# Key and value weights' low parts on VectorE, and the first pair's maxima behind twenty k-steps of the values

## The chip, the cores and the metric

The kernel runs on one core of a Trainium2 chip. The metric is the device time of one execution in microseconds, the median of several runs. The engines are named as in the profile: PE is TensorE (matrix products), PEld its weight loads, DVE is VectorE, ACT is ScalarE, POOL is GpSimd, SP is SyncE, which here issues all loads and stores (DMAs).

## What is computed

Two layers of a diffusion backbone over 512 latent tokens (`L`) and 256 context tokens (`C`), width 1024. Layer 0 mixes tokens by grouped-query attention (16 query heads of 64, 4 heads for keys and values, norm on queries and keys, rotary positions on the latent part); layer 1 by a two-way state-space scan. Each mixer is followed by a gated feed-forward network with a short convolution. The change touches layer 0's attention alone:

```python
q_l, k_l, v_l = jnp.split(h_lat @ w_qkv, [Q_DIM, Q_DIM + KV_DIM], axis=-1)
q_l = rms_norm(q_l.reshape(bsz, seq, N_HEADS, HEAD_DIM), q_norm)
k_l = rms_norm(k_l.reshape(bsz, seq, N_KV_HEADS, HEAD_DIM), k_norm)
...
q_l = apply_rope(q_l, cos, sin)
k_l = apply_rope(k_l, cos, sin)
...
s = jnp.einsum('bqhgd,bkhd->bhgqk', q, k).astype(jnp.float32) * (HEAD_DIM ** -0.5)
p = jax.nn.softmax(s, axis=-1).astype(v.dtype)
return jnp.einsum('bhgqk,bkhd->bqhgd', p, v)
```

## The kernel before

**Products in three parts.** A float32 operand is split into a high part (a rounded copy, type float32r) and a low part (what is left). A product of two operands is three products on PE: high by high, high by low, low by high. `split` (L81) makes the parts: the high one is a cast on ScalarE (L85), the low one a subtraction (L87) on VectorE, or on GpSimd where the caller says `lo_engine="pool"`. `load_w` (L90) loads a block of weights (L95) and splits it; `pin=True` keeps the two instructions in the order in which they are written.

**The stages of the attention.** `attention` runs in this order. (1) Queries and keys of the latent tokens for the first six heads' pairs, tiles `ps_l`. (2) The same for the context, six groups of 24 products, tiles `ps_c`, each copied to `raw0` to `raw5` by ScalarE (L821): `raw0` are the first keys, `raw1` the first queries, `raw2`, `raw4`, `raw5` the next queries, `raw3` the second keys. In between, the two blocks of the values' weights are loaded and split into `wh` and `wl` on ScalarE and GpSimd (L823), and the first keys and queries are prepared. (3) The values: six tiles `ps_v` of 8 k-steps, a k-step being three products (L620); 48 k-steps in all. (4) Eight pairs of query heads, seven steps each: scores (`ps_s`, L796), their shift (L798, with a diagonal matrix `diag` of the row maxima), the exponential on ScalarE (`pr`, L799), sums of `pr` on VectorE (`acc`), and the product with the values (`ps_o`, L760). The next pair's maxima, the next queries' projection (`ps_q`), the modulation (`ps_ada`) and the output projection are woven between these steps.

**Preparing keys and queries.** `normed` (L628 on) squares on ScalarE (L631), scales (L632), sends a copy with swapped rows through a DMA (`qsw`, L635, four loads), sums the squares over a head by products with ones (`ssq`, L640), applies the rotation on VectorE (L642 to L644), and, behind a `yield`, the root (`qy`, L649 and L650 on ScalarE) and the norm (L653 to L655 on VectorE). `keys` (L660) then writes, for each of two heads, tiles `kh` and `kl` in which both halves of 64 partitions hold the same head: `kh` by two casts on ScalarE (L666, L667), `kl` by a subtraction on VectorE for one half (L668) and a cast of it on ScalarE for the other (L669). `queries` (L674) splits into `qh` and `ql`.

**The maxima.** `Pair.maxima` (L714) makes products `ps_m` (L724) in seven groups; VectorE takes each group's maximum (L726, `ma` and `mb`), joins them (L742) and builds `diag` (L747). Without it the shift L798 of the pair's scores cannot run.

**What sets the order.** Each engine works through its own queue in order. From stage 2 on, the queues' order is made by a scheduling layer from the order of the code and its own estimates; an instruction moves ahead of another where nothing binds them, unless it is kept in program order or an edge without a semaphore is added (`add_manual_dep`, as in `follow`). In stage 3 a loop over the 48 k-steps (at the end of `attention`) issues a group of maxima (`m`) every fifth k-step from the first and a part of the second query (`qfirst`) every sixth. PSUM holds two double banks (tag `S`: `ps_s`, `ps_m`) and four single ones (tag `B`: `ps_c`, `ssq`, `ps_v`, `ps_q` and others), so a tile waits until the one that held its bank is read. Weight blocks share ten buffers (`t4`).

Of the kernel before, what the change touches and what calls it, by code (L numbers as in the profile page):

```python
# [7 lines left out]
P = 128  # L8
# [3 lines left out]
ALU = mybir.AluOpType  # L12
# [4 lines left out]
KT = D // P  # L17
# [3 lines left out]
HD = 64  # L21
# [54 lines left out]
def _r(ap):  # L76

    return ap.bitcast(F32)
# [167 lines left out]
def follow(g, bi):  # L246

    if g.last_act is not None:
        g.tc.add_manual_dep(bi.ins, g.last_act.ins.name, mybir.DependencyInfo(
            mybir.DependencyClass.NoSync, mybir.DependencyReason.DATA), reason="order of tables")  # L250
    g.last_act = bi


def ln_exp(g):
# [228 lines left out]
def attention(g, adas, project, X):  # L483


    nc, I = g.nc, g.I
    S64 = slice(0, 64), slice(64, 128)
# [48 lines left out]
    for m in range(KT):  # L536
        sq = t2("sql") if m else acc
# [71 lines left out]
    wv = []  # L609
    vt = [g.t3p.tile([P, NKV * HD], F32, name=f"v{t}") for t in range(T // P)]  # L610

    def values():
        for t in range(T // P):
            h, c0 = (hl, t * P) if t < 4 else (hc, t * P - L)
            ps = Bk("ps_v")
            for k in range(KT):
                w = tuple(w[:, (k % 4) * 256 : (k % 4 + 1) * 256] for w in wv[k // 4])
                ah, al = (a[:, c0 : c0 + P] for a in h[k])
                for i, (s, mv) in enumerate(((ah, w[0]), (ah, w[1]), (al, w[0]))):
                    nc.tensor.matmul(ps[:, :256], s, mv, start=k == 0 and i == 0, stop=k == KT - 1 and i == 2)  # L620
                yield 0.32
            nc.scalar.copy(vt[t], ps[:, :256])

# [4 lines left out]
    def normed(qs, gain):  # L628

        sq = t3(g, "qsq")  # L630
        nc.scalar.activation(sq, qs, AF.Square)  # L631
        nc.scalar.activation(qs, qs, AF.Identity, scale=gain)  # L632
        sw = t2("qsw")
        for b in range(4):
            nc.sync.dma_start(sw[32 * (b ^ 1) : 32 * (b ^ 1) + 32], qs[32 * b : 32 * b + 32, :L])  # L635
        ss = []
        for c0, c1 in ((0, L), (L, T)):
            ps = Bk("ssq")
            for s in S64:
                nc.tensor.matmul(ps[s, : c1 - c0], g.ones[s, :HD], sq[s, c0:c1], start=True, stop=True)  # L640
            ss.append((ps[:, : c1 - c0], slice(c0, c1)))
        nc.vector.tensor_tensor(qs[:, :L], qs[:, :L], g.cos, ALU.mult)  # L642
        nc.vector.tensor_tensor(sw, sw, g.sin, ALU.mult)
        nc.vector.tensor_tensor(qs[:, :L], qs[:, :L], sw, ALU.add)  # L644
        yield

        y, u = t3(g, "qy"), sq
        for ps, c in ss:
            nc.scalar.activation(y[:, c], ps, AF.Ln, scale=1.0 / HD, bias=eps64)  # L649
        nc.scalar.activation(y, y, AF.Exp, scale=-0.5)  # L650
        nc.scalar.activation(u, y, AF.Square)
        for ps, c in ss:
            nc.vector.scalar_tensor_tensor(u[:, c], ps, HD * EPS, u[:, c], ALU.add, ALU.mult)  # L653
        nc.vector.tensor_tensor(qs, qs, y, ALU.mult)
        nc.vector.scalar_tensor_tensor(qs, u, -3.0 * HD, qs, ALU.add, ALU.mult)  # L655
        yield
# [3 lines left out]
    def keys(j, qs):  # L660
        yield from normed(qs, kn)
        for e in range(2):

            h, l = t3(g, f"kh{j}{e}", F32R), t3(g, f"kl{j}{e}", F32R)
            s, o = S64[e], S64[1 - e]
            nc.scalar.copy(h[s], qs[s])  # L666
            nc.scalar.copy(h[o], qs[s])  # L667
            nc.vector.tensor_tensor(l[s], qs[s], _r(h)[s], ALU.subtract)  # L668
            nc.scalar.copy(l[o], _r(l)[s])  # L669
            k2[2 * j + e] = (h, l)  # L670

    qprep = {}
# [34 lines left out]
    class Pair:  # L707
# [6 lines left out]
        def maxima(self):  # L714
# [5 lines left out]
            def scores(ts, k0, n, out):  # L720
                ps = Sb("ps_m")
                for i, t in enumerate(ts):
                    for e in range(2):
                        nc.tensor.matmul(ps[:, 512 * e + n * i : 512 * e + n * i + n], qh[S64[e], t * P : (t + 1) * P],  # L724
                                         kh[S64[e], k0 : k0 + n], start=True, stop=True)
                nc.vector.reduce_max(out[:, :, ts[0] : ts[-1] + 1], ps.rearrange("p (e t k) -> p e t k", e=2, k=n),  # L726
                                     axis=AX.X, negate=True)

# [88 lines left out]
    for n, j in enumerate((0, 1, 2, 4, 5, 3)):  # L817
        ps = Bk("ps_c")
        for k in range(KT):
            k_step(k, j, ps[:, :C], hc)  # L820
        nc.scalar.copy(raw[j][:, L:], ps[:, :C])  # L821
        if n in (1, 3):
            wv.append(load_w(g, I["wv"][len(wv)], lo_engine="pool", pin=True))  # L823
        if n in (1, 2):
            early.append(keys(0, raw[0]) if n == 1 else queries(0, lambda: raw[1]))
        for gen in early:
            next(gen, None)
# [84 lines left out]
    jobs[4].start()  # L912
    m = pairs[0].maxima()
    for i, _ in enumerate(vals):
        if i % 5 == 0:
            next(m, None)
        if i % 6 == 5:
            next(qfirst, None)
        if i == 20:
            wq_split(4)  # L920
# [714 lines left out]
```

## Time and profile before

| | us |
|---|---|
| median of 3 runs | 1904.47 |
| lowest and highest run | 1903.81, 1907.48 |
| the profiled execution | 1906.4 |
| its span, first to last instruction | 1904.2 |
| DVE busy in the span | 1331.0 (70%) |
| ACT busy in the span | 845.4 (44%) |
| POOL busy in the span | 256.9 (13%) |

The profiled execution is one run with the hardware profiler on. All times of single instructions below are from it, in microseconds from the start of the span. A row of a timeline gives start, duration, engine, line of the kernel, operation, output and inputs, shape, count, and in brackets the idle time of the engine before it with what ended it. A row `PE a <- ACT b: 5.5, 1, 5.5` among the waits says that PE waited for ACT before `a`: sum, number, longest. In a table of stretches stand the stretch, its length, each engine's busy time with its count of instructions, the clock that TensorE was granted (1.00 is full) and the DMA's share and GB/s. Matrix products overlap, so their durations add up to more than the time that passes; their distance from start to start is what counts.

The values' stage lies between 91 and 122 us of the span. The second keys (`raw3`) are prepared at about 210 us, among the steps of the third pair.

### The profile page before, as it was taken

Reading aid. Unit: us, or ns where it says so; the run is one execution under the profiler, and the core shown is the slowest. Engines: PE = TensorE matmul, PEld = TensorE weight load, DVE = VectorE, ACT = ScalarE, POOL = GpSimd, SP = SyncE. Lnnn points to the kernel's source line nnn. Section 1 sums busy time; section 2 is a strip of 40 time slices with the busy share of each in tenths; the row PEclk is TensorE's granted clock in tenths of the full one; section 3 lists DMA queues with packets and bytes.
Section 4 is the critical chain, followed back from the end, with each engine's and each line's share of the span. In section 5 each row is a group of like instructions: output and inputs, shape, how many; then the busy total and the mean of one; then the engine's idle time right before and its main releaser. Section 6 shows DMA issues by size and latency. Waiting matters only on the chain.

```text
span 1904.2 us, 27262 instructions
## 1 busy us (share of the span) xinstructions
PE 1864.1 (98%) x10696; PEld 1528.8 (80%) x10696; DVE 1331.0 (70%) x1983; ACT 845.4 (44%) x1454; POOL 256.9 (13%) x238
## 2 busy tenths in 40 slices
PE   8899999989999999999999999999999999999999
PEld 6774545578888888888888888888888888888887
DVE  4478889678877777544478777777878576565555
ACT  3645544355122222222256767766677352323331
POOL 2300000031000000000040334443334200000000
PEclk8999999999999999999999999999999999999999
DMA  9123341014334556221222344344343323323332
GB/s 339 56 67 97 118 157 40 23 56 166 122 122 133 163 189 186 72 67 56 67 89 80 116 122 122 114 131 123 116 130 119 100 78 101 101 86 111 89 99 89
DMA packets 73424, 210.00 MB, mean 110 GB/s; under 512 B 8912, under 2 KB 14416, under 8 KB 73168
## 3 DMA queue, kind: packets, MB, share of 16 engines
q1 hardware_dynamic: 73296, 208.26, 35.1%
q8 instruction: 84, 1.38, 0.3%
q14 instruction: 44, 0.36, 0.1%
HBM read 198.79 MB, written 6.82 MB: 108 GB/s over the span
## 4 chain that ended last, share of the span: by engine, by line
PE 79%; DVE 9%; issue 3%; ACT 3%; DMA 1%; POOL 1%; SPq 0%; DVEq 0%; POOLq 0%; ACTq 0%
PE ps_up L105 10%; PE ps_up L106 10%; PE ps_up L108 10%; PE ps_d L105 6%; PE ps_d L108 6%; PE ps_d L106 6%; PE ps_in L108 4%; PE ps_in L106 4%; PE ps_in L105 4%; PE ps_o L760 2%; PE ps_s L796 2%; PE ps_st L1222 2%; DVE ht L312 1%; PE ps_wo L108 1%; PE ps_wo L105 1%
## 5 line engine op out<-in xcount | busy, mean ns | idle before, releaser
L87 DVE TENSOR_TENSOR wl<-wst,wh 128x1024 fp32r<-128x1024 f32 x209 | 260.3, 1245 | 227.7 <-PE ps_up L106 121.6
L85 ACT CAST wh<-wst 128x1024 fp32r<-128x1024 f32 x211 | 221.2, 1049 | 422.0 <-DMA wst<-in_wup 321.6
L106 PE MATMUL ps_up<-hlf,wh 128*128 128x512 f32 x1008 | 357.2, 354 | 0.0
L108 PE MATMUL ps_up<-hhf,wl 128*128 128x512 f32 x1008 | 356.9, 354 | 0.0
L105 PE MATMUL ps_up<-hhf,wh 128*128 128x512 f32 x1008 | 356.7, 354 | 0.0
L105 PEld LDWEIGHTS ps_up<-hhf,wh 128*128 128x128 f32 x1008 | 190.6, 189 | 26.5
L106 PEld LDWEIGHTS ps_up<-hlf,wh 128*128 128x128 f32 x1008 | 190.7, 189 | 26.3
L108 PEld LDWEIGHTS ps_up<-hhf,wl 128*128 128x128 f32 x1008 | 190.6, 189 | 26.4
L105 PE MATMUL ps_in<-hhs,wh 128*128 128x512 f32 (+1 forms) x560 | 204.5, 365 | 0.0
L106 PE MATMUL ps_in<-hls,wh 128*128 128x512 f32 (+1 forms) x560 | 199.5, 356 | 0.0
L108 PE MATMUL ps_in<-hhs,wl 128*128 128x512 f32 (+1 forms) x560 | 198.8, 355 | 0.0
L105 PE MATMUL ps_d<-hdh,wh 128*128 128x512 f32 (+1 forms) x568 | 193.6, 343 | 1.4 <-DVE X L970 1.2
L108 PE MATMUL ps_d<-hdh,wl 128*128 128x512 f32 (+1 forms) x568 | 193.4, 341 | 0.0
L106 PE MATMUL ps_d<-hdl,wh 128*128 128x512 f32 (+1 forms) x568 | 193.0, 340 | 0.3 <-DVE hdl L87 0.3
L970 DVE SCALAR_TENSOR_TENSOR X<-ps_d,mod,X 128x512 f32<-128x512 f32 (+1 forms) x224 | 125.0, 584 | 34.1 <-PE ps_d L108 33.8
L106 PEld LDWEIGHTS ps_d<-hdl,wh 128*128 128x128 f32 x568 | 106.7, 188 | 14.8 <-DVE hdl L87 0.7
L105 PEld LDWEIGHTS ps_d<-hdh,wh 128*128 128x128 f32 x568 | 106.3, 188 | 14.8 <-DVE X L970 1.4
L105 PEld LDWEIGHTS ps_in<-hhs,wh 128*128 128x128 f32 x560 | 106.0, 189 | 15.1 <-issue 0.9
L108 PEld LDWEIGHTS ps_in<-hhs,wl 128*128 128x128 f32 x560 | 105.9, 189 | 14.8
L108 PEld LDWEIGHTS ps_d<-hdh,wl 128*128 128x128 f32 x568 | 106.7, 188 | 13.1
L106 PEld LDWEIGHTS ps_in<-hls,wh 128*128 128x128 f32 x560 | 106.0, 189 | 13.2
L799 ACT ACTIVATE pr<-ps_s 128x1024 f32<-128x1024 f32 x56 | 57.1, 1020 | 94.0 <-PE ps_s L798 86.7
(355 smaller groups left out, 3506.4 us busy)
## 6 DMA issues: line engine op xcount, KB each, us to landing
wst<-in_wup SPq DMA_DIRECT2D x88, 512.0 KB, 3.6
wada<-in_adaT SPq DMA_DIRECT2D x56, 512.0 KB, 3.7
wst<-in_win SPq DMA_DIRECT2D x48, 512.0 KB, 3.7
wst<-in_wdown SPq DMA_DIRECT2D x44, 512.0 KB, 3.7
E<-ad SPq DMA_DIRECT2D x64, 256.0 KB, 6.7
wada<-in_adaB SPq DMA_DIRECT2D x24, 512.0 KB, 5.0
ec<-ead SPq DMA_DIRECT2D x64, 128.0 KB, 5.1
wst<-in_wout SPq DMA_DIRECT2D x16, 512.0 KB, 3.6
```

The lines of the kernel that those rows point to most:

```text
L85: keep(nc.scalar.copy(hi, src))
L87: keep(eng.tensor_tensor(lo, src, _r(hi), ALU.subtract))
L105: mm(out, wh, ah, start=first, stop=False)
L106: mm(out, wh, al, start=False, stop=False)
L108: mm(out, wl, ah, start=False, stop=last)
L312: nc.vector.scalar_tensor_tensor(t[:, c0:c1], ap, g.moda[layer][ca][:, m, v : v + 1], rs[:, c0:c1], ALU.mult, ALU.mult)
L760: nc.tensor.matmul(po[S64[e], :n], v, pr[:, 512 * e + off : 512 * e + off + n], start=first, stop=last)
L796: nc.tensor.matmul(outs[e], a[S64[e], k], b[S64[e], q], start=i == 0, stop=False)
L799: nc.scalar.activation(pr, ps, AF.Exp)
L970: nc.vector.scalar_tensor_tensor(ap, o[:, c0:c1], gate[:, m, v : v + 1], ap, ALU.mult, ALU.add)
L1222: nc.tensor.matmul(ps[:, d * 256 : (d + 1) * 256], Bt[:, t * P : (t + 1) * P], xw[d][t], start=t == ts[0], stop=t == ts[-1])
```

## The change

Four things are altered. (1) The low parts of the two blocks of the values' weights are made by VectorE and no longer by GpSimd. (2) The second half of each `kl` is made by VectorE from the same sources as the first (one more subtraction, written to the other 64 partitions) and no longer copied by ScalarE; this holds for the first keys and for the second ones. (3) In the values' loop the groups of maxima begin at k-step 19 and come every third k-step, and the parts of the second query begin at k-step 20 and come every seventh. (4) A function `ordered` ties the first pair's `ps_m` and each `ssq` behind the values' product that was issued last in the code; the tie is one of order on PE and adds no semaphore.

```diff
+def ordered(g, bi, prev):
+
+    if prev is not None:
+        g.tc.add_manual_dep(bi.ins, prev.ins.name, mybir.DependencyInfo(
+            mybir.DependencyClass.NoSync, mybir.DependencyReason.DATA), reason="place among products")
...
+    placed = [None]
+
     def values():
...
-                    nc.tensor.matmul(ps[:, :256], s, mv, start=k == 0 and i == 0, stop=k == KT - 1 and i == 2)
+                    placed[0] = nc.tensor.matmul(ps[:, :256], s, mv, start=k == 0 and i == 0, stop=k == KT - 1 and i == 2)
...
-                nc.tensor.matmul(ps[s, : c1 - c0], g.ones[s, :HD], sq[s, c0:c1], start=True, stop=True)
+                ordered(g, nc.tensor.matmul(ps[s, : c1 - c0], g.ones[s, :HD], sq[s, c0:c1], start=True, stop=True), placed[0])
...
             nc.scalar.copy(h[s], qs[s])
             nc.scalar.copy(h[o], qs[s])
-            nc.vector.tensor_tensor(l[s], qs[s], _r(h)[s], ALU.subtract)
-            nc.scalar.copy(l[o], _r(l)[s])
+            for to in (s, o):
+                nc.vector.tensor_tensor(l[to], qs[s], _r(h)[s], ALU.subtract)
...
-                        nc.tensor.matmul(ps[:, 512 * e + n * i : 512 * e + n * i + n], qh[S64[e], t * P : (t + 1) * P],
-                                         kh[S64[e], k0 : k0 + n], start=True, stop=True)
+                        o = nc.tensor.matmul(ps[:, 512 * e + n * i : 512 * e + n * i + n], qh[S64[e], t * P : (t + 1) * P],
+                                             kh[S64[e], k0 : k0 + n], start=True, stop=True)
+                        if self.p == 0:
+                            ordered(g, o, placed[0])
...
-            wv.append(load_w(g, I["wv"][len(wv)], lo_engine="pool", pin=True))
+            wv.append(load_w(g, I["wv"][len(wv)], pin=True))
...
     for i, _ in enumerate(vals):
-        if i % 5 == 0:
+        if i >= 19 and i % 3 == 1:
             next(m, None)
-        if i % 6 == 5:
+        if i >= 20 and i % 7 == 6:
             next(qfirst, None)
```

ScalarE's queue where stage 2 ends, from the last cast of the second weight block on, before the change (`kh00`, `kl00`: first head of the first keys; `kh01`, `kl01`: second head; `ps_c_918` is the context product of `raw5`):

```order
L667 CAST kh00_897<-raw0_713 64x768
L669 CAST kl00_898<-kl00_898 64x768
L666 CAST kh01_903<-raw0_713 64x768
L667 CAST kh01_903<-raw0_713 64x768
L649 ACTIVATE qy_909<-ssq_856,eps64_731 128x512
L649 ACTIVATE qy_909<-ssq_859,eps64_731 128x256
L669 CAST kl01_904<-kl01_904 64x768
L650 ACTIVATE qy_909<-qy_909 128x768
L821 COPY raw5_718<-ps_c_918 128x256
```

The same place in ScalarE's queue after the change, with the changed kernel's line numbers (its L832 is L821 before, L675 and L676 are L666 and L667, L658 and L659 are L649 and L650):

```order
L676 CAST kh00_897<-raw0_713 64x768
L675 CAST kh01_903<-raw0_713 64x768
L676 CAST kh01_903<-raw0_713 64x768
L832 COPY raw5_718<-ps_c_918 128x256
L658 ACTIVATE qy_909<-ssq_856,eps64_731 128x512
L658 ACTIVATE qy_909<-ssq_859,eps64_731 128x256
L659 ACTIVATE qy_909<-qy_909 128x768
L832 COPY raw3_716<-ps_c_948 128x256
```

The two casts of `kl` are gone, and the copy of `raw5` has moved ahead of the root `qy`.

PE's queue in the values' stage, before the change, around the end of the first bank (`ps_v_982` is the first tile of the values, `ps_v_1039` the second; `ps_m_989` the first group of maxima):

```order
L620 MATMUL ps_v_982<-wh_892,hla0_7_117 128x256
L724 MATMUL ps_m_989<-kh00_897,qh_944 128x256 x4
L724 MATMUL ps_m_1011<-kh00_897,qh_944 128x512 x2
L640 MATMUL ssq_1023<-qsq_1015,ones_81 64x512 x2
L640 MATMUL ssq_1026<-qsq_1015,ones_81 64x256 x2
L620 MATMUL ps_v_1039<-wh_791,hha0_0_102 128x256
```

PE's queue after the change, in the middle of the third tile of the values (`ps_v_1034`), where the first group of maxima (`ps_m_1050`) now stands:

```order
L629 MATMUL ps_v_1034<-wh_791,hla0_3_109 128x256
L733 MATMUL ps_m_1050<-kh00_897,qh_944 128x256 x4
L629 MATMUL ps_v_1034<-wh_892,hha0_4_110 128x256
L629 MATMUL ps_v_1034<-wl_893,hha0_4_110 128x256
L629 MATMUL ps_v_1034<-wh_892,hla0_4_111 128x256
L649 MATMUL ssq_1068<-qsq_1060,ones_81 64x512 x2
```

The first maxima have moved from behind the first 24 products of the values to behind the first 60, that is from 8 to 20 k-steps; the second query's `ssq` has moved with them.

VectorE's queue at the second keys (`kl10`, `kl11`, the third pair's steps; `ps_m_2006` a group of the next pair's maxima, `acc_1879` the running sum of `pr`), before the change:

```order
L668 TENSOR_TENSOR kl10_1967<-raw3_716,kh10_1966 64x768
L668 TENSOR_TENSOR kl11_1973<-raw3_716,kh11_1972 64x768
L726 TENSOR_REDUCE ma_1821<-ps_m_2006 128x2
L806 TENSOR_TENSOR acc_1879<-acc_1879,pr_1995 128x1024
L726 TENSOR_REDUCE ma_1821<-ps_m_2033 128x2
```

And after it:

```order
L678 TENSOR_TENSOR kl10_1967<-raw3_716,kh10_1966 64x768 x2
L678 TENSOR_TENSOR kl11_1973<-raw3_716,kh11_1972 64x768 x2
L817 TENSOR_TENSOR acc_1879<-acc_1879,pr_1995 128x1024
L737 TENSOR_REDUCE ma_1821<-ps_m_2006 128x2
L737 TENSOR_REDUCE ma_1821<-ps_m_2033 128x2
```

Two subtractions are added, and the sum now stands ahead of the reduction of `ps_m_2006`. Further on ScalarE's queue, the cast of the sixth pair's query weights (`wh_1327`) stands ahead of the first pair's first `pr`, where it stood behind it; on SP's queue two loads for the modulation (`wada`) stand ahead of the second query's `qsw`, where they stood behind it, and the load of that weight block stands ahead of the third query's `qsw`.

## The prediction

> **What bounds the kernel now.** First the page's first part, then TensorE's waits in the attention (60 to 400 us; sum, times, longest), then the timeline of its longest wait.
>
> ```profile
> PE 1864.1 (98%) x10696; PEld 1528.8 (80%) x10696; DVE 1331.0 (70%) x1983; ACT 845.4 (44%) x1454; POOL 256.9 (13%) x238
> ```
>
> ```profile
> PE ps_v L620 <- ACT raw L821: 5.5, 1, 5.5
> PE ps_ada L128 <- DVE qsq L653: 1.4, 1, 1.4
> ```
>
> TensorE (PE) is busy for 98% of the span, so what is taken off it, or out of its waits, shortens the run, unless another wait takes it up. One wait stands out: the first product of the values (`ps_v`) waits 5.5 us for a copy on ScalarE (ACT). The timeline of PE shows it and what follows (start, duration, engine, line; idle time before it in brackets):
>
> ```profile
> 96.49 0.58 PE L620 MATMUL ps_v<-wh,hha 128*128 128x256 f32 x1 [5.49 <-ACT raw L821]
> ...
> 102.95 1.51 PE L640 MATMUL ssq<-qsq,ones 64*64 64x512 f32 x8 [0.54 <-ACT qsq L631]
> ...
> 118.10 0.28 PE L620 MATMUL ps_v<-wl,hha 128*128 128x256 f32 x1
> ...
> 121.82 0.28 PE L620 MATMUL ps_v<-wh,hla 128*128 128x256 f32 x1
> ...
> 126.74 0.39 PE L724 MATMUL ps_m<-kh,qh 64*128 64x512 f32 x2
> ```
>
> PE has run out of work at 91.0 (96.49 less 5.49). From 118.10 to 121.82 products start every 0.120 us (31 steps). Behind the wait they are slower, as the table of stretches for PE shows (stretch, length, busy time and count, granted clock, DMA):
>
> ```profile
> 96.50:101.00 4.50, 4.50 (x21) 0.50 0.00 0
> 152.00:154.70 2.70, 0.96 (x7) 1.00 0.01 3
> 156.00:157.00 1.00, 1.00 (x8) 0.50 0.41 25
> ```
>
> The clock is halved: 21 products take 0.214 us each (4.50/21) and lose 2.0 us. Now ScalarE's queue, and beside it GpSimd's (POOL) and VectorE's (DVE):
>
> ```profile
> 87.44 0.83 ACT L667 CAST kh<-raw 64x768 fp32r<-64x768 f32 x1
> 90.86 0.83 ACT L669 CAST kl<-kl 64x768 fp32r<-64x768 f32 x1 [2.59 <-DVE kl L668]
> 91.71 0.83 ACT L666 CAST kh<-raw 64x768 fp32r<-64x768 f32 x1
> 92.56 0.83 ACT L667 CAST kh<-raw 64x768 fp32r<-64x768 f32 x1
> 93.40 1.05 ACT L649 ACTIVATE qy<-ssq,eps 128x512 f32<-128x512 f32 x2
> 94.48 0.83 ACT L669 CAST kl<-kl 64x768 fp32r<-64x768 f32 x1
> 95.33 0.84 ACT L650 ACTIVATE qy<-qy 128x768 f32<-128x768 f32 x1
> 96.08 0.35 ACT L821 COPY raw<-ps_c 128x256 f32<-128x256 f32 x1
> ```
>
> ```profile
> 87.55 2.47 POOL L87 TENSOR_TENSOR wl<-wst,wh 128x1024 fp32r<-128x1024 f32 x1 [7.58 <-ACT wh L85]
> 87.67 3.16 DVE L668 TENSOR_TENSOR kl<-raw,kh 64x768 fp32r<-64x768 f32 x1
> 92.57 0.95 DVE L668 TENSOR_TENSOR kl<-raw,kh 64x768 fp32r<-64x768 f32 x1 [1.14 <-ACT kh L666]
> ```
>
> The copy at 96.08 frees the bank that `ps_v` takes. Ahead of it stands L669, waiting 2.59 us for a `kl` on VectorE which took 3.16 us beside GpSimd's `wl`, and 0.95 us when alone.
>
> **The change part by part.** I walk the queues in the new order with the old durations, on the clock of the profiled execution (1906.4 us, span 1904.2; the median of the runs is 1904.47, so a difference is made there and carried over).
>
> *The copy comes earlier.* L669 is gone and the copy of `raw5` stands right behind the key casts: 88.27 (end of L667) plus two casts of 0.83 plus 0.36 gives 90.3. PE is done with `ps_c` at 91.0 and need not stop. The next bank hangs on the copy of `raw3`, behind `qy` (1.05 and 0.84): 92.4, and PE comes at 93.9. **-5.5 us**, and with no stop at 91.0 no half clock: **-2.0 us**. `ssq` finds its square ready (`qh` at 97.7, worked out below, and two instructions of ScalarE behind it: 98.7; PE comes at 99.1): **-0.5 us**.
>
> The second of these terms is the least safe. The rows at 152 to 157 show the clock at 0.50 after a stretch in which PE was busy for 0.96 of 2.70 us and never waited longer than 1.4 us. The Trainium skill, "TensorE: Matmul & The Clock Gate" (What's actually happening), has the clock halved after an idle window of about 3.4 us, on a window that runs freely. By that rule the short waits that I leave below are harmless and the 2.0 us safe; by the rows of 152 to 157 a thin stretch can be enough, and the sum would lose the 2.0 us again.
>
> *VectorE takes over the low parts.* Of the values' weights one wide subtraction falls into an idle gap before 79.72, one stands in the busy queue; of the keys it does both halves now.
>
> ```profile
> 79.72 0.80 DVE L642 TENSOR_TENSOR raw<-raw,cs 128x512 f32<-128x512 f32 x1 [11.16 <-DMA qsw<-raw]
> 99.21 1.22 DVE L87 TENSOR_TENSOR wl<-wst,wh 128x1024 fp32r<-128x1024 f32 x1
> 118.40 0.69 DVE L742 TENSOR_TENSOR mz<-ma,mb 64x6 f32<-64x6 f32 x4
> ```
>
> ```profile
> 96.20:100.35 4.15, 4.00 (x5) 0.50 0.00 0
> 102.20:120.20 18.00, 15.54 (x22) 1.00 0.24 74
> 104.40:122.00 17.60, 17.60 (x136) 1.00 0.30 87
> ```
>
> (The first two are VectorE's stretches, the third is PE's.) In the queue: 1.22 and 2 x 0.95 added, 2.2 of blocking (3.16 less 0.95) gone, net +0.9 us up to the first query. Walked from 87.67: `kl`, `raw1`, `wl` (90.3, needed by PE at 92.5), three more `kl` (92.9), the five instructions of the first stretch (4.0, to 96.9), then the cast `qh` on ScalarE (0.83, to 97.7). Whether a subtraction written to the other 64 partitions costs 0.95 no row shows: at least 0.95 by the straight one, at most 3.16 by the blocked one. I take 0.95, because L742 also writes to the other half and its 64x6 pieces show no extra cost (0.69 for four).
>
> *The maxima move.* Their first product needs `qh`, ready at 97.7. At its old place behind the first bank PE would stand there from 93.9; behind 20 k-steps (60 products, 7.2 us from 91.0) it comes at 98.2 and finds it. Then all seven reductions run in the remaining 28 k-steps. VectorE: the second stretch holds the same work as it will have from the first maximum (98.75) to `diag`, 15.5 us, less 0.9 for a query part that comes before (`ql`), and in my walk 2.25 us of waiting (1.9 for the second maxima, which PE reaches after `ssq`, 0.35 for a square on ScalarE): `diag` done at 115.6. PE: the third stretch, 120 products and six groups of maxima in 17.6 us, gives 0.53 for a group; 84 products, seven groups and `ssq` (1.51) bring PE from 98.2 to 113.5, six scores and the next maxima to 115.0, where it needs `diag`: **+0.5 us**, as uncertain as VectorE's queue is long. Behind that product on PE stand `ssq` of the third query and the first six of `ps_q`, which nothing else waits for yet.
>
> *ScalarE's new order costs a little.* The weight block of the sixth pair's queries is cast (`wh`) ahead of the first `pr` now, not behind it:
>
> ```profile
> 121.74 0.53 SPq L683 DMA_DIRECT2D wst<-in_wq  x1
> 123.26 1.02 ACT L799 ACTIVATE pr<-ps_s 128x1024 f32<-128x1024 f32 x1 [0.75 <-PE ps_s L798]
> 127.29 1.04 ACT L85 CAST wh<-wst 128x1024 fp32r<-128x1024 f32 x1 [3.01 <-DMA wst<-in_wq]
> ```
>
> ```profile
> DMA to landing us min/median/max: 3.6/3.9/5.5
> ```
>
> Its buffer comes free with the last bank's eleventh product, 112.0, and the queue (SP) is idle then, since the next `qsw` load stands behind it. It lands between 115.6 and 117.5; the cast (1.04) and `pr` (1.02) end between 117.7 and 119.6. PE needs this `pr` at 119.3, the place that it reaches at 126.74 before. Cost 0 to 0.3 by that, 0.9 if the load is late once more by half a microsecond; taken as **+0.3 us**. Behind `pr` hangs `raw4` with its `qsw` load (four DMAs); by the same walk it holds VectorE's queue, with the next reduction behind it, but ends 0 to 1.3 us beyond the time at which ScalarE's `qy` lets VectorE go on; none of that is in the sum, it is left to the range. On the queue of loads (SP) two weight blocks of the modulation (`wada`) now stand ahead of the second query's `qsw`; their buffers are free by 96.9, the `qsw` goes out at 99.6, so nothing is held up.
>
> *The second keys.* About 210 us the same edit meets a full VectorE:
>
> ```profile
> 210.43 1.93 DVE L668 TENSOR_TENSOR kl<-raw,kh 64x768 fp32r<-64x768 f32 x2
> 212.39 1.23 DVE L726 TENSOR_REDUCE ma<-ps_m 128x2 f32<-128x1024 f32 x1
> 214.34 1.22 DVE L806 TENSOR_TENSOR acc<-acc,pr 128x1024 f32<-128x1024 f32 x1 [0.72 <-ACT pr L799]
> ```
>
> ```profile
> 215.16 0.40 PE L724 MATMUL ps_m<-kh,qh 64*128 64x512 f32 x2
> ```
>
> Two more `kl` (1.9), and the sum `acc` (1.14) now ahead of the reduction: it ends at 216.5 where the product at 215.16 waits for its bank. **+1.4 us** (0 if VectorE is ahead there by then, 3.0 if both instructions count in full). The casts that ScalarE saves there are worth nothing, as PE does not wait for it.
>
> Sum: -5.5 - 2.0 - 0.5 + 0.5 + 0.3 + 1.4 = **-5.8 us**. 1906.4 becomes 1900.6, the median **1898.7**. What follows is released by PE or by loads whose buffers PE frees, so I see nothing at a fixed time that would swallow it.
>
> **The rivals.**
>
> *VectorE becomes the bound of the values* (0.14). For it: PE already waits 0.5 us for `diag`, so each further microsecond lost in VectorE's queue is lost by PE. Against: the walk already has 2.25 us of waiting in that queue. A slip of 2 to 4 us gives 1900.7 to 1902.7.
>
> *The clock falls all the same* (0.08). If the waits left around `diag` and `pr` make a stretch as thin as that of 152 to 154.7, the 2.0 us come back: 1900.7. Against it: between 98 and 119 my walk leaves PE idle for about 1 us in all.
>
> *The second keys cost nothing* (0.10): 1897.3 or a little less.
>
> *The change does not do what it says* (0.05): PE passes 91.0, but stands at the first maximum for `qh` as long as it stood before. It needs `qh` 5.8 us late; the walk has it 0.5 us early. The result would be the old 1904.5.
>
> *The subtraction across the halves is dear* (0.05), the slower end. Four of them (two before `qh`, two at 210), each extra microsecond paid four times; it decides from 2.4 us each (0.95 plus 5.8/4). At the blocked 3.16 it is 8.8 us more: 1907.5.
>
> **How the numbers follow.** The forecast, 1897.2 to 1900.2, has 0.58. About 0.2% (3.8 us) is what a measurement of this kernel tells from no change: faster means under 1900.7. Faster: nearly all of 0.58, 0.10, a third of 0.14, half of 0.08: 0.74. Slower 0.04, the rest 0.22. The range goes from the -8.0 us of the first three terms with no cost at all, and the 0.66 us by which the lowest of the runs lies under their median (1895.8), to the slip of VectorE at nearly its full 4 us (1902.5); about 0.13 is left out.
>
> **What would show it.** PE's wait for L821's successor gone and `ps_v` at clock 1.00 from its start: steps one and two. First maximum product without a wait: the move. `kl` at about 0.95 in all eight places: VectorE. `diag` waited for by less than a microsecond; `pr` behind the cast `wh` by less than a microsecond. A wait of `ps_m` on a reduction of about 1.4 us near 203 us: the second keys. I am wrong if PE waits over 2 us anywhere between the last `ps_c` and the second pair, or if `kl` to the other half is well over 1 us.

## The result, and the profile after

| | kernel before | changed kernel | ratio (95% interval) |
|---|---|---|---|
| first set of runs (14 and 14) | 1907.38 | 1902.18 | 0.9979 (0.9970 to 0.9989) |
| second set (27 and 10) | 1904.0 | 1898.11 | 0.9972 (0.9961 to 0.9982) |
| third set (21 and 11) | 1902.7 | 1898.69 | 0.9977 (0.9968 to 0.9986) |

The changed kernel is faster by 0.2 to 0.3%: by 5.2, 5.9 and 4.0 us in the medians; by the ratios 4.0 us (2.1 to 5.7) in the first set, 5.3 (3.4 to 7.4) in the second and 4.4 (2.7 to 6.1) in the third. Both kernels together lie up to 5 us lower in the later sets; why one set lies above another is not known. Its profiled execution took 1901.27 us (span 1899.3), 5.1 less than the one that the prediction worked from.

PE is still the bound. First the page's line on busy time, then PE's waits between 60 and 400 us (sum, times, longest), both of the changed kernel:

```profile
PE 1863.7 (98%) x10696; PEld 1526.5 (80%) x10696; DVE 1335.2 (70%) x1989; ACT 841.9 (44%) x1450; POOL 251.3 (13%) x236
```

```profile
PE ps_m L733 <- DVE ma L737: 1.4, 2, 1.2
PE ps_ada L128 <- DVE qsq L662: 1.4, 1, 1.4
...
PE ps_m L733 <- DVE mb L737: 0.8, 1, 0.8
...
PE ps_m L733 <- ACT qh L85: 0.3, 1, 0.3
```

The wait of 5.5 us for the copy on ScalarE is gone; a wait on the reduction `ma` is new (second keys). In the values' stage, timelines of ScalarE, VectorE and PE (L832 is the copy L821 of before, L678 the subtraction L668, L733 the maxima L724, L809 the shift L798):

```profile
88.54 0.84 ACT L676 CAST kh<-raw 64x768 fp32r<-64x768 f32 x1
89.28 0.36 ACT L832 COPY raw<-ps_c 128x256 f32<-128x256 f32 x1
...
96.21 0.84 ACT L85 CAST qh<-raw 128x768 fp32r<-128x768 f32 x1 [2.40 <-DVE raw L664]
```

```profile
86.65 0.94 DVE L678 TENSOR_TENSOR kl<-raw,kh 64x768 fp32r<-64x768 f32 x1
...
89.37 2.89 DVE L678 TENSOR_TENSOR kl<-raw,kh 64x768 fp32r<-64x768 f32 x3
```

```profile
97.48 0.50 PE L733 MATMUL ps_m<-kh,qh 64*128 64x256 f32 x4
...
114.77 0.50 PE L733 MATMUL ps_m<-kh,qh 64*128 64x256 f32 x4 [0.30 <-ACT qh L85]
115.11 0.39 PE L809 MATMUL ps_s<-diag,onesr 64*128 64x512 f32 x2
...
118.89 0.39 PE L733 MATMUL ps_m<-kh,qh 64*128 64x512 f32 x2
```

The copy ends at 89.6, `qh` at 97.1, and the first maximum at 97.48 waits for nothing. The last row is the product that stood at 126.74. This execution was 0.64 us ahead at the end of stage 2 already; net of that the stage has become **7.2 us** shorter.

The saving is followed by taking the same product in two traces and subtracting its starts. The table does so for all profiles of this study (labels are explained with the experiments), always against the first profile of the kernel before; the second column is what a kernel brought along from the start of the run, the fourth is the third less the second.

| profile | last `ps_c` | first pair's scores | gained in the stage | at 165 us | at 180 | at 217 | at 1900 |
|---|---|---|---|---|---|---|---|
| changed | -0.6 | -7.9 | 7.2 | -7.5 | -6.0 | -4.6 | -4.9 |
| changed, e4 | -1.1 | -8.3 | 7.2 | -8.2 | -6.7 | -5.3 | -5.9 |
| changed, a2 | -1.8 | -8.7 | 7.0 | -8.9 | -8.9 | -7.6 | -7.8 |
| e1 | -1.6 | -8.6 | 7.0 | -8.4 | -6.8 | -6.9 | -4.2 |
| e1b | -1.7 | -8.8 | 7.1 | -8.6 | -7.0 | -7.1 | -7.3 |
| f2 | -2.2 | -9.3 | 7.1 | -8.9 | -7.9 | -7.7 | -8.2 |
| e3 | -2.5 | -8.1 | 5.6 | -10.0 | -10.0 | -8.8 | -6.1 |
| e2 | -2.7 | -4.7 | 2.0 | -6.4 | -4.9 | -3.6 | -4.3 |
| e6 | -0.9 | -4.1 | 3.2 | -4.3 | -4.3 | -4.3 | -5.1 |
| e5 | -0.5 | -1.9 | 1.5 | -3.5 | -3.5 | -3.5 | -3.2 |
| e7 | -1.8 | -2.6 | 0.8 | -4.5 | -2.9 | -3.0 | -3.4 |
| before, b1 | -1.2 | -4.0 | 2.8 | -3.9 | -3.9 | -3.9 | -4.2 |
| before, b2 | -1.8 | -1.9 | 0.2 | -1.7 | -0.2 | -0.3 | -1.2 |
| g1 | -0.7 | -3.9 | 3.2 | -5.4 | -3.7 | -3.8 | -3.4 |

Read the first row: 7.2 us gained by 133 us, 0.4 lost again by 160 (at 145 us PE waits 0.76 us for the maximum `mb`, where it waited 0.39 before), 1.5 lost between 165 and 180, 1.4 at the second keys, and nothing of weight in the 1680 us behind. The loss at 165 to 180 was in no step of the prediction, and nothing that the change touches stands there. The tables of stretches show it, first of the changed kernel, then of the kernel before at the same products (stretch, length, busy time and count, granted clock, DMA):

```profile
165.24:168.65 3.41, 2.57 (x14) 1.00 0.00 0
168.65:172.06 3.41, 3.41 (x13) 0.50 0.00 0
```

```profile
173.03:176.44 3.41, 2.85 (x14) 1.00 0.00 0
176.44:179.85 3.41, 3.41 (x19) 1.00 0.00 0
```

In both PE waits 0.84 us for `qsq` there and then runs eight products two columns wide. Behind that the clock was halved in the one and not in the other. The first stretch of each table is one step of a grid on which the clock changes (see the experiments on the scatter), so it holds a little more of PE's work before the change (2.85 us) than after it (2.57). So there were two questions: which part of the change does what, and why executions of one kernel differ.

### The profile page after: what moved, and what is told of

Read it like the earlier page. It is cut to its first block, busy times and chain, and to the rows that moved or that the text cites. A ratio compares the mean times of both kernels' runs of the same rounds, so it can differ in the third digit from the quotient of the medians.

```text
span 1899.3 us, 27264 instructions
## 1 busy us (share of the span) xinstructions
PE 1863.7 (98%) x10696; PEld 1526.5 (80%) x10696; DVE 1335.2 (70%) x1989; ACT 841.9 (44%) x1450; POOL 251.3 (13%) x236
## 4 chain that ended last, share of the span: by engine, by line
PE 80%; DVE 11%; issue 4%; ACT 3%; DMA 1%; POOL 1%; SPq 0%; DVEq 0%; POOLq 0%; ACTq 0%
PE ps_up L105 10%; PE ps_up L106 10%; PE ps_up L108 10%; PE ps_d L105 6%; PE ps_d L108 6%; PE ps_d L106 6%; PE ps_in L108 4%; PE ps_in L106 4%; PE ps_in L105 4%; PE ps_o L771 2%; PE ps_s L807 2%; PE ps_st L1233 2%; DVE ht L319 1%; PE ps_wo L108 1%; PE ps_wo L105 1%
```

## Experiments on the parts

**e2: the maxima back.** The changed kernel without the third and fourth edit:

```diff
-                ordered(g, nc.tensor.matmul(ps[s, : c1 - c0], g.ones[s, :HD], sq[s, c0:c1], start=True, stop=True), placed[0])
+                nc.tensor.matmul(ps[s, : c1 - c0], g.ones[s, :HD], sq[s, c0:c1], start=True, stop=True)
...
-                        if self.p == 0:
-                            ordered(g, o, placed[0])
...
-        if i >= 19 and i % 3 == 1:
+        if i % 5 == 0:
             next(m, None)
-        if i >= 20 and i % 7 == 6:
+        if i % 6 == 5:
             next(qfirst, None)
```

> The changed kernel, with the first pair's maxima and the second query's sum back at their old k-steps and without the ties; the low parts stay on VectorE. Theory A (the move hides the wait for qh): PE reaches the first maxima at 93.1 us (90.2 plus 24 products of 0.120), qh is there at 97.1, so PE stands for some 3.9 us, and the clock falls behind it, another 2 us over some 20 products: 4 to 6 us slower than the changed kernel, about the time of the kernel before. Rival B (the copy of raw5 was all, the move is empty): no wait there, within 0.5 us of the changed kernel.

1903.85 us, 5.7 more than the changed kernel in the same set (expected 4 to 6); ratio 0.9997 (0.9986 to 1.0009) against the kernel before. From PE's timeline:

```profile
95.16 1.22 PE L733 MATMUL ps_m<-kh,qh 64*128 64x256 f32 x6 [4.02 <-ACT qh L85]
```

PE stands 4.0 us for `qh` (expected 3.9), the clock is at half for 6.8 us from 93.5 on, and of the 7.2 us in the stage 2.0 remain. The early copy without the move of the maxima only shifts the stop from one place to the next.

**e3: the low parts of the values' weights on GpSimd again.**

```diff
-            wv.append(load_w(g, I["wv"][len(wv)], pin=True))
+            wv.append(load_w(g, I["wv"][len(wv)], lo_engine="pool", pin=True))
```

> The changed kernel, with the low parts of the values' weights on GpSimd again. Theory A (the copy of raw5 is freed by ScalarE's cast of kl, not by GpSimd): the copy stands at 89 to 90 us as in the changed kernel, and PE does not wait there. The first kl beside GpSimd's subtraction takes about 3.2 us instead of 0.95, VectorE saves one wl of 1.21 ahead of the others, so qh comes about 1.1 us later (98.2) and PE waits some 0.7 us at the first maxima (97.5): 0 to 1 us slower than the changed kernel. Rival B (GpSimd's block on VectorE was the cause): PE waits 2 us or more between the last ps_c and the second tile of the values, and most of the gain of 7 us in this stage is lost.

1900.14 us, ratio 0.9981 (0.9971 to 0.9991). PE does not stop for the copy; at the first maxima it waits 0.58 us (expected 0.7), and another 0.9 us is lost from there to the first pair's scores, where PE's queue has another order (a part of the third query's `ssq` stands ahead of the first `diag` product). 5.6 of the 7.2 us stay. The 1.6 us lost, and the 2.0 us between the medians of the set, are more than the 0 to 1 that I expected. The first `kl` took 0.94 us beside GpSimd's subtraction and not the expected 3.2; here the rotation behind it was the long one (2.89 us).

**e5, e6, e7: one edit alone on the kernel before**: the third and fourth; the first; the second, for the first keys only. Their diffs are the lines of the change's own, for e7 with the second half made by VectorE only where `j` is 0.

> The kernel before with the third and fourth edit alone (maxima and second query's sum at the new k-steps, with the ties); the low parts as before. Compared at the landmark of the first pair's scores (126.7 us in the kernel before), against the kernel before and net of the difference that stands at the last ps_c already. Theory A (every part only moves the wait): PE stands 5.5 us for the copy of raw5 and the clock falls behind it as before; only the 0.5 us for ssq goes: -0.5 us (-1 to +0.5). Rival B (the move alone brings the gain): -3 us or more. The clock: by the profiles so far it falls at the end of a step of a free grid of 3.41 us in which PE was busy for less than about 1.6 us; a fall near 155 us or 176 us must follow such a step here too.

> The kernel before with the first edit alone (the low parts of the values' weights on VectorE). Theory A: the first kl no longer takes 3.2 us beside GpSimd but 0.95, ScalarE's cast of it starts 2.2 us earlier and with it the copy of raw5 (96.1 becomes 93.9): PE's stop at 91.0 shrinks from 5.5 to about 3.2 us, qh comes near 97.5 and PE, 24 products later at 97.1, hardly waits for it: -2 us, and up to 2 us more if the clock then does not fall, net at the first scores. Rival B (ScalarE's cast of kl alone holds the copy, VectorE has nothing to do with it): no change, PE stops for 5 us or more.

> The kernel before with the second edit alone, and for the first keys alone (the other half of kl by VectorE). Theory A: the copy of raw5 stands right behind the casts of kh at 90 us, PE does not stop at 91.0; but GpSimd still holds up the first kl, qh comes at 97 to 98, and PE reaches the first maxima at 93.9: it stands there for 3 to 4.5 us, and the clock falls behind it. Net at the first scores -1 to -3 us. Rival B (the copy of raw5 was the whole loss): -6 us or more.

PE's longest wait between 85 and 130 us in each of the three, in this order:

```profile
PE ps_v L629 <- ACT raw L832: 3.4, 1, 3.4
```

```profile
PE ps_v L620 <- ACT raw L821: 2.9, 1, 2.9
```

```profile
PE ps_m L727 <- ACT qh L85: 5.3, 1, 5.3
```

e6 is as expected: a stop of 2.9 us, 3.2 us gained. e7 confirms that the stop only moves, and even grows (5.3 us at the first maxima, expected 3 to 4.5), so 0.8 us is gained, just short of the 1 to 3. e5 missed: nothing of it touches the copy, and yet PE stopped for 3.4 us and not for 5.5. That opened the question of the race below. Alone, the parts gain 1.5, 3.2 and 0.8 us against the first profile; together 7.2. (The race changes what these numbers mean; see b1 and b2.) The three executions took 1903.23, 1901.02 and 1902.93 us, one each, beside 1903.85 of the kernel before, which is too few to compare.

## Experiments on the second keys

**e1 and e1b** (the same kernel twice): the changed kernel with the old way for the second keys.

```diff
-            for to in (s, o):
-                nc.vector.tensor_tensor(l[to], qs[s], _r(h)[s], ALU.subtract)
+            nc.vector.tensor_tensor(l[s], qs[s], _r(h)[s], ALU.subtract)
+            if j:
+                nc.scalar.copy(l[o], _r(l)[s])
+            else:
+                nc.vector.tensor_tensor(l[o], qs[s], _r(h)[s], ALU.subtract)
```

> The changed kernel, with the second keys (about 203 us) prepared as before the change: the other half of each kl cast by ScalarE, the first keys still by VectorE. Theory A (the second keys cost what the trace after the change shows): PE's wait of 1.4 us for the reduction ma goes, the distance to the kernel before at the landmark behind it grows from 4.6 to 6.1 us, and the run is 1.4 us shorter than the changed kernel: some 1900.8 us in the median. Rival B (VectorE catches up anyway, the wait moves to another instruction): the same wait of 1.2 to 1.4 us stands at another product before 260 us, and the time is that of the changed kernel. Theory C on the clock (PE's clock falls in thin stretches only in some executions): whether it falls near 147 us and near 167 us of the span is not set by this edit; each fall costs 1.5 to 2 us.

> The changed kernel with the second keys as before the change, once more. In its first profile PE waited 2.8 us for GpSimd's hlf at the start of the feed-forward network (430 us; 0.7 us in the changed kernel, with the same order on every engine), which with the clock took back 3.6 us. Theory E' (a race on that place too, not set by the edit): the wait is 0.7 us in this profile or 2.8 again, whatever the time of the run; with 0.7 the span is some 1896 us or less. Rival (the edit shifts the place for good): 2.8 us again. In the median of the runs 1.4 us shorter than the changed kernel, some 1897 to 1899 us.

VectorE's and PE's timelines of the changed kernel, and then VectorE's of e1:

```profile
204.15 3.85 DVE L678 TENSOR_TENSOR kl<-raw,kh 64x768 fp32r<-64x768 f32 x4
208.02 1.22 DVE L817 TENSOR_TENSOR acc<-acc,pr 128x1024 f32<-128x1024 f32 x1
209.17 1.22 DVE L737 TENSOR_REDUCE ma<-ps_m 128x2 f32<-128x1024 f32 x1
```

```profile
210.44 0.49 PE L733 MATMUL ps_m<-kh,qh 64*128 64x512 f32 x2 [1.19 <-DVE ma L737]
```

```profile
203.26 1.93 DVE L677 TENSOR_TENSOR kl<-raw,kh 64x768 fp32r<-64x768 f32 x2
205.22 1.23 DVE L740 TENSOR_REDUCE ma<-ps_m 128x2 f32<-128x1024 f32 x1
```

With the edit the reduction stands behind two more subtractions and the sum, and PE waits; without it the wait is gone and shows up at no other product before 260 us. Between 208 and 217 us the five profiles with the edit on the second keys (the changed kernel's three, e2, e3) lose 1.3 to 1.5 us, all others at most 0.1. In the runs this is too little to be seen: 1897.31 us (6 runs) beside 1898.11 for the changed kernel in the same set, and 1898.29 (11) in a set without it; the ratios to the kernel before, 0.9963 (0.9949 to 0.9977) and 0.9974 (0.9965 to 0.9983), overlap with those of the changed kernel. The wait of 2.8 us at 430 us, which the expectation of e1b speaks of, is taken up at the end.

## Experiments on the scatter

**e4: the changed kernel, no edit.**

> The changed kernel, unaltered, for a second profile. Theory C (the fall of the clock in a thin stretch depends on when it comes, not on the instructions): the stretch at 165 to 173 us has the same instructions and waits in both profiles so far, and lost 1.5 us after the change and nothing before it. A second profile may show it with or without; if without, it is 1.5 us shorter up to there (distance to the kernel before 7.5 instead of 6.0 us at 180 us). Rival D (the change itself makes the clock fall there): the clock falls at 167.5 to 172.5 us again, here and in every kernel that keeps the change's order ahead of it.

1898.11 us. Its clock fell at 167.87 us, and 1.5 us were lost again; a third profile of the same kernel (a2, below) lost nothing there, and b2, the kernel before, lost 1.5. So rival D falls, and theory C stands: the place is hit in some executions of either kernel. In all 15 profiles the clock changes only on a grid of 3.413 us, which stands elsewhere in each execution: in the first profile of the kernel before it fell at 94.52 and 155.96 (61.44, or 18 steps apart), in that of the changed kernel at 148.17 and 168.65 (20.48, 6 steps). At two thin places, of which f2 alone alters one, the fall goes with PE's busy time in the step of the grid ahead. Near 147 us of the changed kernel, steps with up to 1.77 us busy were followed by half clock in 10 cases of 11, steps with 1.99 or more in none of 4; that is a fall in 10 of 15 profiles. Near 166 us, the fall came in 8 of 10 profiles where the step held the whole gap (2.57 us busy, the narrow products counted in), and in none of 5 with 2.64 or more. As the two places have different limits, busy time as the profile counts it is not the whole rule. The limits that I wrote into expectations (1.4 to 1.65 us) were too narrow. A fall at 166 costs 1.5 to 1.6 us.

The Trainium skill, "TensorE: Matmul & The Clock Gate" (What's actually happening), has a free-running window of 3413 ns; these traces agree to the third digit. It speaks of an idle window; here half a window of work was not enough.

**f2: the gap at 166 us partly filled.** e1 with six products of the third pair's maxima repeated ahead of the wait (the same values, written again), and the narrow products behind the wait tied behind them:

```diff
-        nc.tensor.matmul(pt[:, 2 * i : 2 * i + 2], sb[:, i * P : (i + 1) * P], g.sel, start=True, stop=True)
+        ordered(g, nc.tensor.matmul(pt[:, 2 * i : 2 * i + 2], sb[:, i * P : (i + 1) * P], g.sel, start=True, stop=True), g.fill)
...
+                for j in range(6 if self.p == 2 and ts == (0, 1) else 0):
+                    i, e = j // 2 % 2, j % 2
+                    g.fill = nc.tensor.matmul(ps[:, 512 * e + n * i : 512 * e + n * i + n],
+                                              qh[S64[e], ts[i] * P : (ts[i] + 1) * P], kh[S64[e], k0 : k0 + n], start=True, stop=True)
                 nc.vector.reduce_max(out[:, :, ts[0] : ts[-1] + 1], ps.rearrange("p (e t k) -> p e t k", e=2, k=n),
```

> The same kernel with six products of 256 columns repeated (one group of the third pair's maxima, the same values written again) ahead of the wait of 0.84 us that stands at 166 us, where the clock has fallen in six of nine profiles. Theory C (the clock falls after a step of 3.41 us with PE busy for less than some 1.5 us): the gap there shrinks from 1.8 to 1.1 us and the clock no longer falls at 165 to 173 us; as the fall costs 1.5 us in two runs of three, the mean is 1 us shorter than without the repeats and the spread smaller. Rival (the products only cost PE's time): the fall comes as often, and the run is 0 to 0.7 us longer.

(The count there should read five of nine.) The clock did not fall at 166, but 6 of 14 profiles without the filling do not fall either, and 1.2 us were lost between 165 and 217 all the same (beside the repeats, VectorE's queue has another order there). 1897.0 us (6 runs), ratio 0.9969 (0.9957 to 0.9980), against 1898.29 for e1b in the same set: inconclusive.

**b1 and b2: the kernel before, no edit.**

> The kernel before, unaltered, for a second profile. Theory E (a race behind the stop): with GpSimd making the second weight block's low part, the first kl takes 3.2 us where GpSimd begins 0.12 us ahead of it (kernel before) and 0.94 where the two begin within 0.03 us or kl begins first (three experiments; the rotation behind it then takes 2.9). In the first case PE stops 5.5 us for the copy of raw5, in the second 3.4 us, as where only the maxima were moved. So this profile shows either 3.2 and 5.5 or 0.95 and 3.4, and the place of the first pair's scores moves with it by about 2 us. Rival F (the first profile is what this kernel always does): 3.2 and 5.5 again.

> The kernel before, unaltered, for a third profile. As for the second: theory E (a race) allows either 3.2 us for the first kl with a stop of 5.5 us, or 0.95 with 3.4; rival F has 3.2 and 5.5 in every profile. The clock falls after a step of the 3.41 us grid in which PE was busy for less than 1.4 us, and not where it was busy for over 1.65.

One of each; the two executions took 1902.21 and 1905.22 us. The timelines of GpSimd and VectorE and PE's longest wait (85 to 130 us), of b1 and then of b2:

```profile
86.34 3.21 POOL L87 TENSOR_TENSOR wl<-wst,wh 128x1024 fp32r<-128x1024 f32 x1 [7.58 <-ACT wh L85]
86.33 0.94 DVE L668 TENSOR_TENSOR kl<-raw,kh 64x768 fp32r<-64x768 f32 x1
87.20 2.89 DVE L644 TENSOR_TENSOR raw<-raw,qsw 128x512 f32<-128x512 f32 x1
```

```profile
PE ps_v L620 <- ACT raw L821: 3.3, 1, 3.3
```

```profile
85.80 2.64 POOL L87 TENSOR_TENSOR wl<-wst,wh 128x1024 fp32r<-128x1024 f32 x1 [7.58 <-ACT wh L85]
86.10 3.15 DVE L668 TENSOR_TENSOR kl<-raw,kh 64x768 fp32r<-64x768 f32 x1
89.17 0.68 DVE L644 TENSOR_TENSOR raw<-raw,qsw 128x512 f32<-128x512 f32 x1
```

```profile
PE ps_v L620 <- ACT raw L821: 5.7, 1, 5.7
```

Theory E holds: where GpSimd begins 0.12 us (the first profile) or 0.30 us (b2) ahead, the first `kl` is blocked and ScalarE's cast of it, and so the copy, come late. Where the two begin within 0.03 us of each other (b1, e5, e7), or VectorE 0.43 ahead (e3), `kl` takes 0.94 us and the block falls on the rotation (L644), which nobody on ScalarE waits for yet. VectorE's start hangs on the `qsw` load (it waited 1.06 us for it in b1, 1.37 in b2), GpSimd's on a cast. The outcomes differ by 2.6 us in the stage (2.8 and 0.2 in the table). The first profile, from which the prediction was made, and b2 are of the dear kind (stops of 5.5 and 5.7 us), b1 of the cheap one (3.3). In b1 the half clock behind the stop is shorter as well; from the table of stretches of b1 and then of the first profile:

```profile
93.06:96.47 3.41, 3.35 (x15) 0.50 0.00 0
```

```profile
94.52:101.34 6.82, 4.85 (x22) 0.50 0.00 0
```

This bears on the parts. e5 and e7 ran with the cheap outcome and were compared with a first profile of the dear one. Against b1, which stands 2.8 us ahead unaltered, e5 is 1.3 us and e7 2.0 us behind at the first pair's scores, e6 is 0.4 ahead and the whole change 4.4 (one profile each). So what looked like a gain of the third and fourth edits alone, and of the second alone, was the race.

**g1: the race decided for `kl`, and a2, the changed kernel beside it.** In the kernel before, the second block's load and cast are written out at their place, and GpSimd reads an element of `kl` ahead of its second subtraction:

```diff
...
+        if n == 3:
+            g.tc.keep_in_program_order(nc.gpsimd.tensor_copy(first_kl, _r(k2[0][1])[0:1, 0:1]))
+            g.tc.keep_in_program_order(nc.gpsimd.tensor_tensor(wl, st, _r(wh), ALU.subtract))
```

> The kernel before with GpSimd's subtraction for the second weight block held back until VectorE's first kl is written (GpSimd reads one element of it first); the order on all other engines is unaltered. Theory E (race): kl takes 0.95 us in the profile, PE stops for 3.0 to 3.6 us instead of 5.5, and the runs lose their upper part: the median is 1 to 2.5 us under that of the kernel before, and no more than 1 run in 10 is over 1905. Rival F (the scatter of the kernel before has another source): stop and kl as said, but the median and the spread are those of the kernel before less at most 0.5 us.

> The changed kernel once more, in the same set as the kernel before with the race forced. Theory E: the change saves against that kernel only what the order makes, some 4.4 us in the values' stage less 1.4 at the second keys: 3 us (2 to 4); against the kernel before as it is 4 to 5.5. Rival F: 5 us or more against both.

VectorE's first `kl` and GpSimd's subtraction in g1:

```profile
86.40 0.94 DVE L668 TENSOR_TENSOR kl<-raw,kh 64x768 fp32r<-64x768 f32 x1
```

```profile
87.95 2.39 POOL L836 TENSOR_TENSOR wl<-wst,wh 128x1024 fp32r<-128x1024 f32 x1
```

`kl` takes 0.94 us, PE stops for 2.9, and the stage is 3.2 us shorter than in the first profile. 1901.6 us against 1902.7: 1.1 less, at the low end of what theory E gave, and the ratio, 0.9995 (0.9986 to 1.0004), does not exclude nothing. The upper part of the runs is gone (highest 1903.78 of 11; 7 of 21 of the kernel before lie over 1904), but over the expectation's own line of 1905 lie only 2 of 21 of the kernel before, so that line tells little. Against g1 the changed kernel saves 2.9 us, against the kernel before 4.0: E's numbers, where F asked for 5 or more against both. That the race sets the stop and the length of the stage is shown by g1's profile; that it shifts the median of the runs is supported and not shown, and how often it goes which way in a set is not known.

## Why the prediction was right, and where it was wrong

Its walk through the queues came out in the traces nearly to the tenth (its times less the 0.64 us that this execution was ahead):

- *The copy*: expected to end at 89.7, ended at 89.6; no stop, `ps_v` at clock 1.00. Right. By e7 the second edit alone is enough for this, but e2 and e7 show that the stop then stands at the first maxima; the gain takes the edits together.
- *The first query and the maxima*: `qh` expected at 97.1, was there at 97.1; the first maximum expected at 97.6, came at 97.48, without a wait, and `ssq` waits for nothing either (the -0.5). Right. The rival "stands at the first maximum" is what e2 does.
- *The subtraction across the halves*: 0.96 us each (2.89 for three). Right; the rival "dear" fell.
- *VectorE as the bound*: the first `diag` product at 115.1 against 115.0; no wait for `diag` shows there, only 0.3 us for `qh` in the product ahead, so the +0.5 had about the right size and the wrong cause. *ScalarE's order* (`wh` ahead of `pr`): the landmark behind both stands at 118.89, where -7.2 us put it. So the stage's sum was right for this execution, 7.2 expected and 7.2 measured; the +0.3 was not measured by itself.
- *The second keys*: expected +1.4, measured 1.3 to 1.5 in five profiles, none in the others.

Wrong was the last step: "1906.4 becomes 1900.6, the median **1898.7**", with the remark that a difference made in the profiled execution is carried over to the median of the runs. The forecast was 5.8 us less than a median of 1904.47; the sets gave 4.0 to 5.3 by the ratios, and 1902.18 as the first median. Three things fail in it.

First, the base. The median of the three runs shown was 1904.47; over the 14 runs of the first comparison the same kernel has 1907.38. That is 2.9 of the 3.5 us by which 1902.18 lies over the forecast. That the other sets have 1898.11 and 1898.69, on the forecast, is luck: there the kernel before stands at 1904.0 and 1902.7, and how much lower a set lies was in no step. Luck, too, is that 1902.18 lies inside the stated range: its upper part was meant for a slip of VectorE, which did not come.

Second, the size of the first two terms (-5.5 for the stop, -2.0 for the clock behind it). This is the step that fails in the prediction's own sum. They are what one execution lost, one in which GpSimd had won by 0.12 us (87.55 against 87.67, both quoted in the prediction, and not read as a race). In b1 the stop is 3.3 us, and behind it 15 products run at half clock where the first profile has 22, which is a loss of some 1.4 us by the prediction's own figures (0.214 less 0.120 us each). The two terms are 4.7 us there instead of 7.5, and the whole sum would be -5.8 plus 2.8, or -3.0. The ratios of the three sets, 4.0, 5.3 and 4.4 us, lie between the two, though the interval of each set is wide enough to reach at least one of them.

Third, "nothing at a fixed time that would swallow it". Something without a fixed time did: in this execution the grid of the clock lay so that the thin place at 166 us cost 1.5 us, which the profile of before had not paid. My rival "the clock falls all the same" looked for that in the changed stretch, where the clock held; the place that was hit is untouched and takes its toll from both kernels, and which execution pays goes mostly by where the grid lies in it.

With the falls at 166 left out, the profiled executions give -7.2 + 1.4 = -5.8 us, and another 0.4 us went between 133 and 160 (the longer wait for `mb`). The mechanism of the stage was right; the size belongs to executions of the dear kind.

## What to carry to other kernels

Before a wait is booked as a gain, look at what starts within a few tenths of a microsecond of its cause: a stop that hangs on which of two engines came first is worth only its mean over executions, and one profile cannot give that. Follow a saving by the distance between the same products in two traces; it tells in one table where it was made, and what took some of it back. Of an edit that is applied in two places, price each place: the first keys' edit was needed, the second keys' cost 1.4 us in the traces. By that, the kernel with the first alone (e1) should be the best of those here that do no extra work; the runs do not separate it from the changed kernel. And a part that is measured alone must be compared with a profile in which the race fell the same way.

## What the runs showed of the hardware

- A start of 0.12 us or more ahead decided who was blocked when GpSimd and VectorE both ran wide subtractions: 0.94 or 3.15 us for the same `kl`. The Trainium skill, "Trainium Architecture — The Big Picture" (What this means for kernel authors), calls the port that these two share an exclusive lock; the rows agree. A second place with two outcomes stands at the start of the feed-forward network: in e1 (and in e3) GpSimd's four `hlf` ran as one stretch of 5.93 us, in e1b, the same kernel as e1, as two of 1.87 and 2.48. There the starts do not tell the two apart: GpSimd began 0.11 us behind VectorE's `ht` in e1 as in e1b, so what decides at this place is not shown. PE's waits between 400 and 450 us, of e1 and then of e1b:

```profile
PE ps_first L106 <- POOL hlf L326: 3.6, 3, 2.8
```

```profile
PE ps_first L106 <- POOL hlf L326: 1.5, 3, 0.7
```

- The start of the run depends on the same grid: the seven profiles with four steps at half clock between 10 and 27 us stand 0 to 1.2 us ahead of the first one at the last `ps_c`, the eight with three steps 1.6 to 2.7. With the race (2.6 us) and the falls at 166 (1.5) that is of the order of the scatter among the runs of the kernel before, 7 us in the first set; that the runs without a profile differ for the same reasons is argued, not shown.
